# Dividing the attention keys into two parts where they are computed

## The chip, the cores and the metric

One core of one Trainium2 chip runs the kernel. The metric is device time in microseconds, from the first to the last instruction of one execution; several runs give a median. One more execution is taken with the hardware profiler, and it is the source of all rows below.

## The reference

The kernel computes one layer of a hybrid block for 1024 latent tokens and 256 context tokens of width 1024, all in float32. What matters here is the attention branch, with 8 heads:

```python
kv = (rms_norm(ckv, kv_norm_g) @ w_ukv).reshape(b, l, N_HEADS, QK_NOPE_DIM + V_HEAD_DIM)
k_nope, v = jnp.split(kv, [QK_NOPE_DIM], axis=-1)
...
k = jnp.concatenate([k_nope, k_pe], axis=-1)
...
s = jnp.einsum('bhqd,bhkd->bhqk', qi, k).astype(jnp.float32) * scale
p = jax.nn.softmax(s, axis=-1).astype(v.dtype)
return jnp.einsum('bhqk,bhkd->bhqd', p, v)
```

A head has 128 columns of k_nope and 64 rotated columns k_pe, which all heads share. Every latent token reads the 1280 keys of all tokens. Beside the attention there is a state-space branch (S5) with gates, and after both a retrieval layer (PEER): each token chooses 128 of 16384 experts, each a row of `peer_u` (scores) and a row of `peer_v` (values).

## The kernel before

**Numbers in two parts.** A score is a product of float32 numbers. The kernel forms it from parts in a shorter format (F32R): `split` (L230) casts x to a high part on ACT (L232) and subtracts it from x on an engine, VectorE by default, to get the low part (L233). A product is then three matmuls: high with high, low with high, high with low. In `attention`, L857 to L859 do so for the queries and the keys without rotation, and L860 and L861 add the rotated part from `kpe_h` and `kpe_l`, which are divided once, in `compress` (L688, L689).

**Stages.** First the S5 branch is computed, interleaved with the compression of all tokens (`compress`), the values (`values`) and the keys (`keys`). `keys(h, c0, c1)` (L701) makes one stretch of 512 or 256 keys of head h: two matmuls into a PSUM bank (L704), a copy to SBUF on ACT (L707), a store to the DRAM tensor `k_d` issued on ACT's queue (L708). There are 24 such calls. Their small buffers, tag `kv`, are a ring of 3 that `values` and earlier steps also use. PSUM tiles of the tag `mm` alternate between two banks at most.

Then the 8 tiles of 128 latent tokens go through in four groups, of 1, 2, 3 and 2 tiles (`GROUPS`, L42). A group's `front` (L1402) runs attention, gates, the output projection with its norms (`close`), and hands back the generator of its retrieval choice (`route`), whose steps are taken between the heads of the next group's attention (`TSTEP`, two steps per head). The gathers of expert rows for tiles 0 and 1 (`score`, L1269 and L1273; `weighted`, L1349 and L1354), which POOL issues, are emitted after the last front, with a lower priority, and fill in beside groups 1 to 3. Tiles 2 to 5 are served at the end by a dense stage over all experts (L1233 to L1235, L1194 to L1196), with the gathers of tiles 6 and 7 beside it.

**Attention, head by head.** For each pair of heads the query weight is loaded and the queries computed (L816 to L830). For each head the 1280 keys are loaded from `k_d` (L837), by `wload` (L203), into the ring W: 4 buffers of 8 KB per partition that are handed out in program order, for query weights, keys, the retrieval's query weights (L1052) and gate weights alike. A buffer is free again when the last reader of its former load is done. Then the keys are divided in three stretches (L839 to L844) into six tiles, one buffer each, in the pool of the attention; the values are loaded into a ring of two (L846); and for each token tile come the 15 score matmuls, three maxima on VectorE (L862), three exponentials on ACT (L871), and, one step later, transposes and the product with the values (`finish`, L795).

**The order.** All loads are issued on SP's queue, stores mostly on ACT's; each queue and engine works in order. The order within each is set when the program is built, by a scheduler that simulates a timeline, with priorities (`PRIO`, L69). Tiles of a pool have fixed addresses; a tile may be filled when whatever held these addresses before has been read for the last time, so that the attention pool's loads wait for pools that were released before it.

Of the kernel before, what the change touches and what calls it, by code (L numbers as in the profile page):

```python
# [8 lines left out]
F32 = mybir.dt.float32  # L9
F32R = mybir.dt.float32r  # L10
# [7 lines left out]
MUL, ADD, SUB = ALU.mult, ALU.add, ALU.subtract  # L18
# [4 lines left out]
KEYS = 1280  # L23
# [58 lines left out]
KENG = ((), (), (), ())  # L82
# [6 lines left out]
def block_kernel(ctx: ExitStack, tc: tile.TileContext, a: dict, out: bass.AP):  # L89
# [35 lines left out]
    k_d = tc.dram_tile([8, 128, KEYS], F32, name="k_d")  # L125
# [104 lines left out]
    def split(hi, lo, x, eng=V):  # L230

        S.copy(hi, x)  # L232
        eng.tensor_tensor(lo, x, hi.bitcast(F32), op=SUB)  # L233
# [39 lines left out]
    mrow = pre.tile([128, 512], F32, tag="kv", bufs=3, name="mrow")  # L273
# [27 lines left out]
    def project(n):  # L301
# [25 lines left out]
        su = pre.tile([128, 4, 128], F32, tag="kv", bufs=3, name="su")  # L327
# [363 lines left out]
    def values(n):  # L691
        for h in range(2):
            ps = bank("mm", "pv")
            for k in range(2):
                PE.matmul(ps, ckvT[:, k, n * 128:(n + 1) * 128], wk[k][:, 1024 + h * 512:1536 + h * 512],
                          start=(k == 0), stop=(k == 1))
            vt = pre.tile([128, 512], F32, tag="kv", bufs=3, name="vt")
            S.copy(vt, ps)
            S.dma_start(v_d[4 * h:4 * h + 4, :, n, :].rearrange("h p d -> p h d"), vt.rearrange("p (h d) -> p h d", h=4))

    def keys(h, c0, c1):  # L701
        ps = bank("mm", "pk")
        for k in range(2):
            PE.matmul(ps[:, 0:c1 - c0], wk[k][:, h * 128:(h + 1) * 128], ckvT[:, k, c0:c1],  # L704
                      start=(k == 0), stop=(k == 1))
        kt = pre.tile([128, 512], F32, tag="kv", bufs=3, name="kt")
        S.copy(kt[:, 0:c1 - c0], ps[:, 0:c1 - c0])  # L707
        S.dma_start(k_d[h, :, c0:c1], kt[:, 0:c1 - c0])  # L708
# [79 lines left out]
    def attention(grp, att):  # L788
# [22 lines left out]
        for pr in range(4):  # L811
# [19 lines left out]
            for hh in range(2):  # L831
# [5 lines left out]
                kt = wload(k_d[h], [128, KEYS])  # L837
                kc = []
                for c in range(3):  # L839
                    c0, w = 512 * c, (512 if c < 2 else 256)  # L840
                    kh = A.tile([128, w], F32R, tag="kh%d" % c, name="kh")
                    kl = A.tile([128, w], F32R, tag="kl%d" % c, name="kl")
                    split(kh, kl, kt[:, c0:c0 + w], GP if c in KENG[GROUPS.index(grp)] else V)
                    kc.append((kh, kl))  # L844
# [745 lines left out]
```

## Time and profile before

| what | us |
|---|---|
| median of 3 runs | 3764.03 (3756.9 to 3764.93) |
| profiled execution, its own time | 3758.78 |
| span of the profiled execution, first to last instruction | 3757.0 |
| mean granted TensorE clock in it | 0.946 of full speed |

Engines are PE (matmul), PEld (its weight loads), DVE (VectorE), ACT (ScalarE), POOL (GpSimd) and SP (which only issues loads). Busy time is the time in which an engine executes. "a <- b: 12.3, 4" in a list of waits says that a's instructions sat idle for 12.3 us in 4 cases until b was done. The chain is followed back from the last instruction to what released each piece of work. A piece of it shows its start, its length in us and what it was; "issue" is time without a visible cause.

### The profile page before, as it was taken

How to read it: one execution, taken by the hardware profiler on the slowest of the kernel's cores; microseconds unless marked ns; L12 is line 12 of the kernel's file. 1: busy time of each engine (PE TensorE's matmuls, PEld its weight loads, DVE VectorE, ACT ScalarE, POOL GpSimd, SP SyncE). 2: the span in 40 equal slices, each digit the busy share in tenths (PEclk: the TensorE clock that was granted, in tenths of full speed). 3: DMA queues.
4: the chain of work that ended last, by engine and by line, in shares of the span. 5: the costliest groups of instructions: out<-in, count | busy, mean ns of one | idle time of the engine just before them, and what ended most of it. 6: DMA issues, size and time to landing. Idle time of an engine off the chain costs nothing.

```text
span 3757.0 us, 54909 instructions
## 1 busy us (share of the span) xinstructions
PE 3376.1 (90%) x20022; PEld 2741.5 (73%) x20022; DVE 2889.2 (77%) x6864; ACT 1496.5 (40%) x2967; POOL 1477.3 (39%) x1254
## 2 busy tenths in 40 slices
PE   5968888979779889879989879999999999999997
PEld 3745577869667669667659668788888888888885
DVE  7357755685898877789846667888888888889985
ACT  2223353443123457133359794333333333333332
POOL 5035400041355553454441300465555555546530
PEclk7978999989889989989999989999999999999998
DMA  8652276476698888887887854699999999989972
GB/s 279 230 87 72 89 263 225 157 296 244 230 341 312 311 334 334 339 325 286 292 328 272 323 206 163 236 359 339 343 336 337 332 335 339 340 319 355 338 272 73
DMA packets 348718, 1032.49 MB, mean 275 GB/s; under 512 B 46592, under 2 KB 142080, under 8 KB 322592
## 3 DMA queue, kind: packets, MB, share of 16 engines
q0 software_dynamic: 147456, 536.94, 39.0%
q1 hardware_dynamic: 164032, 462.20, 34.7%
q10 hardware_dynamic: 36960, 29.86, 2.5%
q8 instruction: 157, 2.57, 0.3%
q14 instruction: 113, 0.93, 0.1%
HBM read 961.27 MB, written 67.62 MB: 274 GB/s over the span
## 4 chain that ended last, share of the span: by engine, by line
PE 56%; DVE 9%; issue 7%; DMA 5%; ACT 4%; POOL 2%; SPq 0%; DVEq 0%; ACTq 0%; POOLq 0%
PE turn L1233 6%; PE turn L1234 6%; PE turn L1235 6%; PE fd L1194 5%; PE fd L1195 5%; PE fd L1196 5%; DMA ub<-in_peer_u,ei 2%; PE pqr L1065 2%; DVE ub L1273 2%; PE acc L1354 2%; PE pe L1151 2%; DMA vb<-in_peer_v,eiT 2%; PE po L808 2%; PE po L953 1%; POOL ub L1269 1%
## 5 line engine op out<-in xcount | busy, mean ns | idle before, releaser
L1269 POOL DMA_INDIRECT ub<-in_peer_u,ei x512 | 639.6, 1249 | 1221.7 <-DVE ub L1273 446.8
L1273 DVE SCALAR_TENSOR_TENSOR ub<-ub,h 128x1024 f32<-128x1024 f32 x512 | 617.0, 1219 | 52.4 <-DMA ub<-in_peer_u,ei 46.5
L1316 POOL DMA_INDIRECT vb<-in_peer_v,ei x256 | 363.4, 1420 | 266.3 <-DVE f L1319 203.6
L1349 POOL DMA_INDIRECT vb<-in_peer_v,eiT x256 | 288.4, 1126 | 402.8 <-PE acc L1354 313.5
L1233 PE MATMUL turn<-hh,u 128*128 128x512 f32 x1024 | 400.9, 392 | 1.2 <-ACT act L1237 1.2
L1234 PE MATMUL turn<-hh,u 128*128 128x512 f32 x1024 | 400.5, 391 | 0.1
L1235 PE MATMUL turn<-hl,u 128*128 128x512 f32 x1024 | 399.9, 390 | 0.0
L1195 PE MATMUL fd<-v,kpe_l 128*128 128x512 f32 x891 | 353.5, 397 | 3.6 <-DVE kpe_l L233 3.6
L1196 PE MATMUL fd<-v,kpe_h 128*128 128x512 f32 x891 | 351.1, 394 | 0.0
L1194 PE MATMUL fd<-v,kpe_h 128*128 128x512 f32 x891 | 341.5, 397 | 0.0
L1319 DVE SCALAR_TENSOR_TENSOR f<-vb,zz,f 128x1024 f32<-128x1024 f32 x254 | 325.7, 1282 | 3.1 <-DMA vb<-in_peer_v,ei 0.4
L1237 ACT ACTIVATE act<-turn 128x512 f32<-128x512 f32 x128 | 76.6, 598 | 588.0 <-PE turn L1235 587.9
L232 ACT CAST v<-w 128x1024 fp32r<-128x1024 f32 x128 | 134.8, 1053 | 282.9 <-PE fd L1195 279.4
L1233 PEld LDWEIGHTS turn<-hh,u 128*128 128x128 f32 x1024 | 192.2, 188 | 44.1 <-ACT act L1237 1.4
L1235 PEld LDWEIGHTS turn<-hl,u 128*128 128x128 f32 x1024 | 192.3, 188 | 41.9
L1234 PEld LDWEIGHTS turn<-hh,u 128*128 128x128 f32 x1024 | 192.2, 188 | 41.1 <-DVE u L233 0.4
L1354 PE MATMUL acc<-vb,diag 128*32 128x256 f32 x2048 | 164.5, 402 | 49.0 <-DMA vb<-in_peer_v,eiT 45.8
L1148 DVE TENSOR_SCALAR second<-iota,pl 128x128 f32<-128x128 f32 x512 | 141.4, 350 | 81.4 <-PE pe L1151 74.7
L1195 PEld LDWEIGHTS fd<-v,kpe_l 128*128 128x128 f32 x891 | 167.5, 188 | 43.4 <-DVE kpe_l L233 4.6
L1196 PEld LDWEIGHTS fd<-v,kpe_h 128*128 128x128 f32 x891 | 167.6, 188 | 41.5
L1194 PEld LDWEIGHTS fd<-v,kpe_h 128*128 128x128 f32 x891 | 167.3, 188 | 40.7
L233 DVE TENSOR_TENSOR v<-w,v 128x1024 fp32r<-128x1024 f32 x128 | 156.6, 1223 | 43.4 <-ACT v L232 42.7
(422 smaller groups left out, 8254.2 us busy)
## 6 DMA issues: line engine op xcount, KB each, us to landing
w<-in_peer_uT SPq DMA_DIRECT2D x64, 1024.0 KB
w<-in_peer_v SPq DMA_DIRECT2D x64, 1024.0 KB
w<-in_peer_wq SPq DMA_DIRECT2D x32, 1024.0 KB
gT_d<-stage SPq DMA_DIRECT2D x16, 2048.0 KB
gt<-gT_d SPq DMA_DIRECT2D x32, 1024.0 KB
vh<-v_d SPq DMA_DIRECT2D x32, 640.0 KB
w<-k_d SPq DMA_DIRECT2D x32, 640.0 KB
w<-in_w_mod_b SPq DMA_DIRECT2D x16, 1024.0 KB
```

Of the source, the lines that this page charges most:

```text
L1194: PE.matmul(o, ah[:, ts], vh[:, cs], start=first, stop=False)
L1195: PE.matmul(o, al[:, ts], vh[:, cs], start=False, stop=False)
L1196: return PE.matmul(o, ah[:, ts], vl[:, cs], start=False, stop=final)
L1233: PE.matmul(turn, uh[:, k, :], hh[:, k, :], start=(k == 0), stop=False)
L1234: PE.matmul(turn, ul[:, k, :], hh[:, k, :], start=False, stop=False)
L1235: PE.matmul(turn, uh[:, k, :], hl[:, k, :], start=False, stop=(k == 7))
L1269: GP.indirect_dma_start(out=ub, out_offset=None, in_=a["peer_u"], in_offset=bass.IndirectOffsetOnAxis(ap=ei[:, s:s + 1], axis=0))
L1273: V.scalar_tensor_tensor(ub, ub, 1.0, h2, op0=MUL, op1=MUL, accum_out=dots[:, s:s + 1])
L1316: GP.indirect_dma_start(out=vb, out_offset=None, in_=a["peer_v"], in_offset=bass.IndirectOffsetOnAxis(ap=ei[:, s:s + 1], axis=0))
L1319: V.scalar_tensor_tensor(f, vb, z[:, s:s + 1], f, op0=MUL, op1=ADD)
L1349: GP.indirect_dma_start(out=vb, out_offset=None, in_=a["peer_v"], in_offset=bass.IndirectOffsetOnAxis(ap=eiT[:, t:t + 1], axis=0))
L1354: PE.matmul(acc[d // 2][o:o + 32, 256 * (d % 2):256 * (d % 2) + 256], dg[:, q, jj, :], vb[:, d * 256:(d + 1) * 256], start=False, stop=Fal ...
```

## The change

`keys` now makes two tiles per call: ACT casts the PSUM bank into the high part, VectorE subtracts it from the bank into the low part, and both are stored, so that `k_d` has a dimension of 2 and twice the size. The ring `kv` grows to 4 buffers. In `attention` the six tiles and their casts and subtractions are gone. In groups 0 to 2 (`KTB`, which takes the place of `KENG`) one load per head fetches both parts into a ring of two tiles of its own, in the attention's pool: 20 KB per partition where the six tiles had 10 KB. In group 3 two loads per head fetch the parts into two buffers of the ring W, and the matmuls read them there.

```diff
-KENG = ((), (), (), ())
+KTB = (2, 2, 2, 0)
...
-    k_d = tc.dram_tile([8, 128, KEYS], F32, name="k_d")
+    k_d = tc.dram_tile([8, 128, 2, KEYS], F32, name="k_d")
...
-            vt = pre.tile([128, 512], F32, tag="kv", bufs=3, name="vt")
+            vt = pre.tile([128, 512], F32, tag="kv", bufs=4, name="vt")
...
-        kt = pre.tile([128, 512], F32, tag="kv", bufs=3, name="kt")
-        S.copy(kt[:, 0:c1 - c0], ps[:, 0:c1 - c0])
-        S.dma_start(k_d[h, :, c0:c1], kt[:, 0:c1 - c0])
+        for z in range(2):
+            kt = pre.tile([128, 512], F32, tag="kv", bufs=4, name="kt")[:, 0:c1 - c0]
+            if z:
+                V.tensor_tensor(kt.bitcast(F32R), ps[:, 0:c1 - c0], kh, op=SUB)
+            else:
+                kh = kt
+                S.copy(kt.bitcast(F32R), ps[:, 0:c1 - c0])
+            S.dma_start(k_d[h, :, z, c0:c1], kt)
...
-                kt = wload(k_d[h], [128, KEYS])
-                kc = []
-                for c in range(3):
-                    c0, w = 512 * c, (512 if c < 2 else 256)
-                    kh = A.tile([128, w], F32R, tag="kh%d" % c, name="kh")
-                    kl = A.tile([128, w], F32R, tag="kl%d" % c, name="kl")
-                    split(kh, kl, kt[:, c0:c0 + w], GP if c in KENG[GROUPS.index(grp)] else V)
-                    kc.append((kh, kl))
+                ktb = KTB[GROUPS.index(grp)]
+                if ktb:
+                    kt = A.tile([128, 2, KEYS], F32R, tag="kt", bufs=ktb, name="kt")
+                    SY.dma_start(kt.bitcast(F32), k_d[h])
+                    kt = kt[:, 0], kt[:, 1]
+                else:
+                    kt = [wload(k_d[h, :, z], [128, KEYS]).bitcast(F32R) for z in range(2)]
+                kc = [[x[:, c:min(c + 512, KEYS)] for x in kt] for c in range(0, KEYS, 512)]
```

## Rows read from the trace of the kernel before

**Rows 1.** The page, busy us (share of the span) xinstructions of each engine.

```profile
PE 3376.1 (90%) x20022; PEld 2741.5 (73%) x20022; DVE 2889.2 (77%) x6864; ACT 1496.5 (40%) x2967; POOL 1477.3 (39%) x1254
```

**Rows 2.** Windows: from:to, length, busy PE PEld DVE ACT POOL, PEclk, DMA share, GB/s.

```profile
290.00:430.00 140.00, 122.63 (x645) 76.59 (x644) 116.29 (x169) 48.94 (x123) 86.12 (x98) 0.88 0.23 69
430.00:475.00 45.00, 37.80 (x187) 24.34 (x186) 28.97 (x48) 18.05 (x42) 5.81 (x4) 1.00 0.40 134
...
488.00:550.00 62.00, 56.35 (x377) 51.01 (x375) 35.21 (x99) 39.64 (x105) 0.00 (x0) 0.93 0.71 250
...
640.00:805.00 165.00, 142.46 (x958) 126.84 (x957) 122.36 (x467) 72.83 (x207) 23.24 (x20) 0.96 0.53 188
...
1000.00:1305.00 305.00, 255.34 (x1845) 205.86 (x1843) 273.64 (x948) 100.19 (x262) 164.64 (x151) 0.93 0.88 323
...
1765.00:1915.00 150.00, 139.66 (x1114) 99.96 (x1116) 118.86 (x543) 54.15 (x139) 67.31 (x64) 0.97 0.81 286
...
2400.00:3000.00 600.00, 595.99 (x2569) 481.64 (x2568) 523.70 (x715) 198.85 (x270) 349.04 (x255) 1.00 0.94 339
```

**Rows 3.** The chain that ended last, shares by line.

```profile
by line: issue 7.4%; PE turn L1233 6.0%; PE turn L1234 5.9%; PE turn L1235 5.9%; PE fd L1194 5.3%; PE fd L1195 5.3%; PE fd L1196 5.3%; DMA ub<-in_peer_u,ei 2.5%; PE pqr L1065 2.5%; DVE ub L1273 2.4%; PE acc L1354 2.0%; PE pe L1151 1.9%; DMA
```

**Rows 4.** Tile kh: xcount: ns min/median/max, first and last start us, forms.

```profile
L232 ACT CAST kh<-w x96: 399/618/660, 488.9 to 1891.5; 128x512 fp32r<-128x512 f32 x64, 128x256 fp32r<-128x256 f32 x32
L233 DVE TENSOR_TENSOR kl<-w,kh x96: 409/681/736, 489.6 to 1893.7; 128x512 fp32r<-128x512 f32 x64, 128x256 fp32r<-128x256 f32 x32
```

**Rows 5.** Tile kt, its stores; and the page's DMA issues, KB each.

```profile
L708 ACTq DMA_DIRECT2D k_d<-kt x24: 326/336/462, 300.9 to 472.6; - x24
...
w<-k_d SPq DMA_DIRECT2D x32, 640.0 KB
```

**Rows 6.** Lines 689 and 604 alone, columns as in group 4.

```profile
L689 DVE TENSOR_TENSOR kpe_l<-pt,kpe_h x5: 278/292/292, 321.6 to 447.6; 128x128 fp32r<-128x128 f32 x5
...
L604 DVE TENSOR_TENSOR gi<-w1t,w2t x8: 824/1027/1885, 235.3 to 455.3; 128x640 f32<-128x640 f32 x8
```

**Rows 7.** The chain in group 1, pieces with keys: start us, us, what.

```profile
647.16 1.44 ACT kh L232 x3
...
681.31 4.14 DMA w<-k_d
...
686.00 0.92 ACT kh L232 x2
...
732.63 3.98 DMA w<-k_d
...
766.16 0.66 DVE kl L233
...
770.47 0.33 DVE kl L233
```

**Rows 8.** DVE's groups, 1000 to 1305 us: xcount | busy, mean ns | idle before.

```profile
L1273 DVE SCALAR_TENSOR_TENSOR ub<-ub,h 128x1024 f32<-128x1024 f32 x106 | 128.5, 1217 | 8.9 <-DMA ub<-in_peer_u,ei 8.6 <-issue 0.2
```

**Rows 9.** The chain in group 2, first and last of six kl pieces.

```profile
1068.72 0.59 DVE kl L233
...
1150.31 0.34 DVE kl L233
```

**Rows 10.** Waits of SP's queue, 475 to 2270 us: total, times, longest.

```profile
SPq L213 <- DVE kl L233: 137.6, 13, 31.0
```

**Rows 11.** Waits of DVE and of PE for gathered rows, 475 to 2270 us.

```profile
DVE ub L1273 <- DMA ub<-in_peer_u,ei: 34.1, 25, 4.5
...
PE acc L1354 <- DMA vb<-in_peer_v,eiT: 45.8, 21, 7.0
```

**Rows 12.** The window with the highest rate of those read, columns as in group 2.

```profile
1520.00:1565.00 45.00, 37.62 (x189) 29.81 (x188) 26.45 (x65) 1.19 (x2) 13.46 (x13) 0.89 0.92 351
```

**Rows 13.** Group 1's first value loads on SP; its first score matmuls on the chain.

```profile
647.14 0.80 SPq L846 DMA_DIRECT2D vh<-v_d  x2
...
657.47 0.59 PE pS L857 x3
```

More of the change, by code (lines that the diff above doesn't have):

```diff
@@ L272, in block_kernel @@
         SY.dma_start(ldt[64 * d:64 * d + 64, :], a["s5_log_dt"][d].partition_broadcast(64))
-    mrow = pre.tile([128, 512], F32, tag="kv", bufs=3, name="mrow")
+    mrow = pre.tile([128, 512], F32, tag="kv", bufs=4, name="mrow")
     GP.memset(mrow, 0.0)
@@ L326, in project @@
                 PE.matmul(pc[:, b, :], w1[:, k, b * 128:(b + 1) * 128], hm[:, k, :], start=(k == 0), stop=(k == 7))
-        su = pre.tile([128, 4, 128], F32, tag="kv", bufs=3, name="su")
+        su = pre.tile([128, 4, 128], F32, tag="kv", bufs=4, name="su")
         S.copy(su, pc)
```

## The prediction

> **What bounds the kernel now.** I read the busy line first: PE has the largest share, 90%, DVE 77%, ACT 40% [rows 1]. An average says little here, so I cut the span into stages [rows 2]; a reader should look for the engine whose busy time comes nearest to the stretch's own length. Keys are made up to 475 us; there DVE has 29.0 of the last 45 us. The four attention stages follow: group 0 (488 to 550), group 1 (640 to 805), group 2 (1000 to 1305) and group 3 (about 1625 to 1915). Group 0 is PE's, 56.4 of 62 us. Group 1 is PE's with DVE close, 142 and 122 of 165 us, and its DMA moves only 188 GB/s. Group 2 is DVE's, 273.6 of 305 us, at a DMA share of 0.88. The last part of group 3 is PE's again, 139.7 of 150 us. After that comes the dense stage, in which PE is never idle (596 of 600 us). Then the chain of what ended last [rows 3]: its largest lines are the dense stage's matmuls; gathers and the score multiplication of L1273 follow; nothing of the keys' division reaches the list. The change touches nothing in the dense stage, so all that it can win or lose lies before it.
>
> **What is removed.** 96 casts kh on ACT (median 0.618 us) and 96 subtractions kl on DVE (0.681 us), two thirds 512 and one third 256 wide [rows 4]. Per group that is 24 of each: 16 x 0.681 + 8 x 0.41 = 14.2 us of DVE, and 16 x 0.618 + 8 x 0.40 = 13.1 us of ACT. Over four groups DVE loses 57 us and ACT 52 us. ACT is not the fullest engine in any of these stages [rows 2], so its 52 us count only where they stand on the chain.
>
> **What is added.** In the keys' stage, per call one more DVE subtraction from PSUM and one more store. The 24 stores are issued on ACT's queue at 0.336 us [rows 5], 8 us on an engine busy 18 of 45 us. In the attention, every head reads 1280 KB in place of 640 KB [rows 5]: 5.24 MB more per group, 21 MB over four, and 5.24 MB more written once.
>
> **Keys' stage.** 16 subtractions of 512 and 8 of 256: 14.2 us by the durations of kl [rows 4]. No row shows this one exactly. The nearest is L689, the same operation with one input from PSUM, 128 wide: 0.278 to 0.292 us, five times, without spread [rows 6]. In the same stage L604, with both inputs in SBUF, goes from 0.824 to 1.885 us [rows 6], so another kind of DVE work is stretched there. Taking L689 as the nearer, I keep 14.2 us; stretched like L604's median against its minimum (1.25 times) it would be 18, like its maximum (2.3 times) 33. In the last 45 us DVE has 16 us free; before that it has 24 of 140 [rows 2]. The PSUM bank of each call is also held until the subtraction ends, and the next matmul of that bank waits for that. I put under half of it on the path: **+6 us**, bounds 0 (all in DVE's free time) and +23 (most of the stretched case).
>
> **Group 0.** Its casts and subtractions lie beside PE, which leaves 62 - 56 = 6 us to win at most. The loads go from 250 GB/s x 62 us = 15.5 MB to about 20.7 MB, 60 us at the 345 GB/s that the fullest stretches show (mean of 339 and 351 [rows 2, 12]). The next limit is as near as the old one: **0 us**, bounds -6 and +6.
>
> **Group 1.** Here the chain does touch the keys [rows 7]: twice it waits for a key load, 4.14 and 3.98 us, each time with 0.92 us of casts behind it; 1.44 us of casts stand on it at the first head, and three pieces of kl, 1.6 us, near the end. 8.1 + 1.8 + 1.4 + 1.6 is about 13 us. The load was late because it needs one of four buffers that it shares with the query and retrieval weights; in a ring of its own, two heads deep, it starts a head earlier. What is late next is the value tile, which needs its ring too, or the route's matmuls, which already fill this stage. The first head is a place for a loss: value tiles, in the same pool as the new key tiles, are only issued at 647.14 [rows 13], and a key tile of twice the bytes takes some 8 us by rows 7, to 655; the first score matmul starts at 657.47 [rows 13]. It is covered with 2 us to spare. I take **-12 us**, bounds -13 and 0.
>
> **Group 2.** DVE is full, and 106 score multiplications of L1273 (128.5 us) share it with kl [rows 8]. Only two heads' kl, six pieces and 3.1 us, stand on the chain [rows 9]; but in an in-order queue that is 90% full the other pieces push what does. Between 3.1 and 14.2 us, nearer to the full engine: **-8 us**. Against it, 5.24 MB at 345 GB/s are 15.2 us of transfer, of which the stage has (345 - 323) x 305 us = 6.7 MB free. They fit, just. Bounds -14 and +8 (15.2 less the DVE time that goes).
>
> **Group 3.** The keys stay in the shared ring, as two tiles per head, kept until the head's last score matmul and no longer only until kl. kl and kh are not on the chain in this stage, PE is the fullest. I take **0 us**; bounds -6 (part of DVE's 14.2 while heads share it with routing) and +28 (the second rival).
>
> **The load queue.** On SP's in-order queue, loads into the shared ring waited 137.6 us in all for kl [rows 10]. In groups 0 to 2 this wait goes; the keys' own load will then wait for score matmuls two heads back, which is earlier in the queue than it bites. The chain shows no weight load that was late for it, so I count nothing.
>
> **Sum.** 6 + 0 - 12 - 8 + 0 = -14 us against the profiled execution's 3758.8 us (span 3757.0), or 3745. That execution stands 5.2 us under the median of the runs, 3764.0; on the median the sum gives 3750 us. Measurements of this kernel can tell about 0.2%, 7.5 us, from no change.
>
> **Rival one: the transfers take the gain back.** Before, DVE waited 34.1 us for gathered rows in its multiplications and PE 45.8 us for those of L1354, over groups 0 to 3 [rows 11]; both engines work in order, so a late row holds the attention behind it. The 15.7 MB of groups 1 to 3 are 46 us of transfer. If the DMA is what sets groups 2 and 3, group 2's -8 becomes 0 or more and group 3 adds a few: 6 - 12 + 0 + 4 = -2, that is 3762 us, no change. For it: shares of 0.81 to 0.92 and stretches at 339 to 351 GB/s and none higher [rows 2, 12]. Against it: group 1, with the surest gain, has 188 GB/s. In the Trainium skill, HBM Reference, section Specifications, a core's share is given as about 358 GB/s and a core alone as about 425; the trace, at 351, shows nothing above the share. By 425 group 2 would have 31 MB free instead of 6.7 and this rival would fall; by 358 it stands.
>
> **Rival two: the shared ring of group 3 (slower).** With two of four buffers per head, and two retrieval weights loaded between heads, the next head's key tile falls on the buffer of the last one, and can't be issued before its last score matmul; the next query weight likewise. A load costs the chain at least the 4.1 us of rows 7. Seven head changes: 7 x 4.1 = 28 us, and -14 becomes +14, or 3778 us. It decides once PE and DVE have less than 4 us of other work queued at each change. For it: nothing is prefetched across heads any more. Against: the routing of group 2 and the weighted rows of L1354 lie between heads and are PE's larger part here.
>
> **Rival three: the keys' stage pays in full.** +23 in place of +6 makes 3767, no change; with group 2 at 0 it is 3775, slower.
>
> **How the numbers follow.** Forecast, gains in groups 1 and 2: 0.44. Rival one 0.25; two 0.19; three 0.12, of which 0.02 stays within 0.2% and 0.10 is slower. So faster 0.44, same 0.27, slower 0.29. The range for 8 in 10 goes from 3722 (-42: nearly all lower bounds together, -6 - 13 - 14 - 6 = -39) to 3790 (rival two with one more bound, or three with part of two). The forecast's own range is 3722 to 3756.
>
> **What would show it.** Right: in the changed profile kh and kl are gone from the attention; the first score matmul of group 1 stands no later after its queries; no chain piece waits for a key load in group 1; group 2's stretch from first to last head is some 8 us shorter with the DVE busy time down by 14; the last k_d store and the start of group 0 are some 6 us later. Wrong: head-to-head gaps in group 3 with PE waiting on a load; DMA waits at L1273 and L1354 grown by more than 10 us; a dense stage that starts less than 8 us sooner than before.

## The result and the profile after

The changed kernel takes **3779.1 us** in the median (3774.7 to 3786.1, 6 runs), against 3759.1 us (3756.4 to 3764.9, 6 runs) for the kernel before on the same chip: a ratio of 1.0051, 95% interval 1.0033 to 1.0068. By the ratio it is slower by about 19 us, where 14 us of gain were forecast. Its profiled execution took 3777.1 us, with a span of 3774.7 us, 17.7 us above the span of before.

What the change was to do, it did. The page of the changed kernel, and, for the last line, its list of DMA issues:

```profile
PE 3378.2 (89%) x20022; PEld 2745.0 (73%) x20022; DVE 2849.5 (75%) x6792; ACT 1448.7 (38%) x2869; POOL 1471.0 (39%) x1254
...
kt<-k_d SPq DMA_DIRECT2D x24, 1280.0 KB
...
w<-k_d SPq DMA_DIRECT2D x16, 640.0 KB
```

Against [rows 1], DVE has 40 us less to do, ACT 48 us, PE the same. The 40 are roughly the 57 us of kl less the some 14 us that the subtraction in the keys' stage adds (tile kt of the changed kernel; ns min/median/max, first and last start):

```profile
L709 DVE TENSOR_TENSOR kt<-pk,kt x24: 418/678/692, 299.0 to 473.6; 128x512 fp32r<-128x512 f32 x16, 128x256 fp32r<-128x256 f32 x8
```

So the time was lost by work that waits, not by work that was added. I cut both spans at the same events of their timelines: the last matmul pa (end of the first query compression), a group's last `att` on ACT, the last matmul of `close`, the first `turn` of the dense stage. The numbers in this table are differences of those times, so each column adds up to its span. "Before, again" is a second profile of the same kernel on another chip (e5, the chip of e6) and shows how far one profile can be trusted: rows differ by up to 6 us. e1 and e2 ran on a third chip, on which the median of the kernel before is 3744.1 us, 15 us less; so a column of theirs can be read for where time moved, and not to the last few us against "before".

| stretch, us | before | before, again | changed | e1 | e2 | e6 |
|---|---|---|---|---|---|---|
| to the end of pa | 480.4 | 482.6 | 484.8 | 477.0 | 479.9 | 480.5 |
| to the end of group 0's attention | 91.2 | 89.1 | 99.9 | 89.4 | 99.9 | 96.8 |
| to the end of group 1's attention | 285.8 | 284.2 | 260.8 | 267.1 | 264.8 | 283.2 |
| to the end of group 1's close | 98.7 | 97.2 | 128.3 | 125.1 | 114.2 | 98.7 |
| to the end of group 2's close | 621.0 | 627.1 | 599.5 | 623.0 | 596.7 | 615.6 |
| to the end of group 3's close | 539.8 | 538.9 | 546.9 | 533.4 | 530.0 | 537.5 |
| to the dense stage | 153.4 | 150.9 | 173.0 | 156.6 | 167.9 | 147.9 |
| dense stage to the end | 1486.7 | 1483.8 | 1481.5 | 1483.4 | 1487.4 | 1489.3 |

In the changed kernel the attention of group 1 and all of group 2 are faster, by 25 and 21.5 us. Four stretches give more than that back: group 0 (+9), group 1's gates and close (+30), group 3 (+7) and what lies before the dense stage (+20). Group 3's 7 us are hardly more than the spread of the rows; the other three can be read in views.

**Group 0.** First the kernel before, SP's timeline (start us, us, what) and PE's (in brackets the idle time before it and what ended it); then the changed one, in the same order:

```profile
481.73 0.42 SPq L213 DMA_DIRECT2D w<-in_w_uq  x1
```

```profile
487.53 2.90 PE L820 MATMUL pq<-cqT,w 128*128 128x128 f32 x12 [2.30 <-issue]
```

```profile
479.03 0.48 SPq L845 DMA_DIRECT2D kt<-k_d  x1
479.56 0.42 SPq L851 DMA_DIRECT2D vh<-v_d  x1
480.03 0.43 SPq L845 DMA_DIRECT2D kt<-k_d  x1
...
489.38 5.05 SPq L213 DMA_DIRECT2D w<-in_w_uq  x4
```

```profile
501.32 5.28 PE L825 MATMUL pq<-cqT,w 128*128 128x128 f32 x24 [12.05 <-issue]
```

Now keys of two heads, in a ring of their own and so free to go, stand ahead of the first query weight, with the values and tables that used to follow it, and the queries start 14 us later; counted from the end of pa it is 9 us (16.5 in place of 7.1).

**Group 1.** ACT's timeline of the kernel before, then of the changed one, at the casts of the gates' inputs:

```profile
795.90 1.05 ACT L232 CAST hm<-w 128x1024 fp32r<-128x1024 f32 x1
804.07 1.04 ACT L232 CAST hm<-w 128x1024 fp32r<-128x1024 f32 x1 [3.16 <-DMA w<-hm_d]
```

```profile
845.49 1.05 ACT L232 CAST hm<-w 128x1024 fp32r<-128x1024 f32 x1
846.96 1.04 ACT L232 CAST hm<-w 128x1024 fp32r<-128x1024 f32 x1
866.41 1.90 ACT L232 CAST w<-w 128x2048 fp32r<-128x2048 f32 x1 [17.89 <-DMA w<-in_w_gm]
```

The last `att` of group 1 ends at 857.4 us in the first and at 845.5 in the second. Before, the casts were done over 50 us ahead of it; now the first one begins in the moment in which it ends. The attention's pool has become 10 KB longer and reaches into the addresses of the gates' pool, so the gates' tiles can be filled only when the attention is done. SP's timelines, before and changed, show what that does to the queue; the changed kernel's list of SP's waits, 800 to 860 us, and the waits of all engines, 820 to 900 us, show the price:

```profile
801.23 0.34 SPq L213 DMA_DIRECT2D w<-in_w_gm  x1
...
820.11 0.33 SPq L213 DMA_DIRECT2D w<-in_w_gm  x1
...
855.33 0.33 SPq L757 DMA_DIRECT2D hm<-hm_d  x1
```

```profile
845.22 0.32 SPq L762 DMA_DIRECT2D hm<-hm_d  x1
...
849.13 0.33 SPq L213 DMA_DIRECT2D w<-in_w_gm  x1
```

```profile
SPq L762 <- PE po L813: 32.1, 1, 32.1
```

```profile
PE pg L238 <- ACT w L232: 23.2, 1, 23.2
ACT w L232 <- DMA w<-in_w_gm: 17.9, 1, 17.9
```

The load L762, L757 before (for the next group's queries), waits for the attention's end in both kernels. Before, two of the gates' weights w_gm went out ahead of it. Now they stand behind it, and PE sits idle for 23 us in front of the gates. Read by itself, the attention of this group misleads: it is shorter because the gates' loads and casts no longer run beside it (e1 shows the same without any change of the keys).

**Group 2 and the rows behind it.** The attention went as forecast (the line of `att` in its group, before and after: 326 and 316 us from first to last):

```profile
L809 ACT ACTIVATE att<-po,smx x24: 350/368/373, 1023.0 to 1348.6; 128x128 f32<-128x128 f32 x24
```

```profile
L814 ACT ACTIVATE att<-po,smx x24: 367/367/386, 1030.3 to 1346.2; 128x128 f32<-128x128 f32 x24
```

But beside it DVE has to score 92 gathered rows of tile 0 in one stretch. DVE's groups in that stretch, before (985.3 to 1165.2 us) and after (1003.4 to 1201.2 us):

```profile
L1273 DVE SCALAR_TENSOR_TENSOR ub<-ub,h 128x1024 f32<-128x1024 f32 x92 | 111.1, 1216 | 5.0 <-DMA ub<-in_peer_u,ei 4.7 <-issue 0.2
L862 DVE TENSOR_REDUCE mx<-pS 128x1 f32<-128x512 f32 (+1 forms) x30 | 17.4, 593 | 2.9 <-PE pS L861 2.9
...
L994 DVE FIND_INDEX8 I<-V,sc 128x8 uint32<-128x128 f32 x19 | 5.3, 284 | 0.0
```

```profile
L1278 DVE SCALAR_TENSOR_TENSOR ub<-ub,h 128x1024 f32<-128x1024 f32 x92 | 111.1, 1215 | 5.1 <-DMA ub<-in_peer_u,ei 4.8 <-issue 0.3
L867 DVE TENSOR_REDUCE mx<-pS 128x1 f32<-128x512 f32 (+1 forms) x36 | 20.2, 592 | 7.1 <-PE pS L866 7.1
...
L999 DVE FIND_INDEX8 I<-V,sc 128x8 uint32<-128x128 f32 x24 | 6.7, 284 | 0.0
```

The rows cost the same 111.1 us and wait the same 5 us for their gathers. There is more other work between them: 36 maxima for 30, 24 searches of L999 for 19. The attention and the choice of experts go ahead, the score rows fall behind: they take 198 in place of 180 us. They end 36 us later, and the other half of that is their later start, with group 1's close 18 us late. The weighted rows (L1354, now L1359) come behind them through the same six buffers and the same queue on POOL. Their matmuls from 1640 us on, before and after:

```profile
L1354 PE MATMUL acc<-vb,diag x1344: 379/379/636, 1652.5 to 2165.1; 128*32 128x256 f32 x192
```

```profile
L1359 PE MATMUL acc<-vb,diag x1392: 376/379/637, 1646.6 to 2242.5; 128*32 128x256 f32 x199
```

They end 77 us later, 123 in place of 49 us after group 3's close, and the dense stage starts 23 us later (its first matmuls, before and after):

```profile
L1233 PE MATMUL turn<-hh,u x77: 387/389/504, 2270.3 to 2399.9; 128*128 128x512 f32 x77
```

```profile
L1238 PE MATMUL turn<-hh,u x62: 389/389/628, 2293.2 to 2400.0; 128*128 128x512 f32 x62
```

Much of the 20 us ahead of it is PE's work that used to be done earlier. PE's groups of row matmuls between group 3's close and the dense stage, before (2116.9 to 2270.3 us) and after (2120.2 to 2293.2):

```profile
L1354 PE MATMUL acc<-vb,diag 128*32 128x256 f32 x188 | 14.5, 390 | 2.6 <-DMA vb<-in_peer_v,eiT 2.5
```

```profile
L1359 PE MATMUL acc<-vb,diag 128*32 128x256 f32 x368 | 29.4, 411 | 7.2 <-DMA vb<-in_peer_v,eiT 6.1 <-issue 1.1
```

These are 180 more, 15 us of PE; 48 of them used to be done in group 2's stretch of the table and 132 in group 3's. DVE's work is put off too. The stretches of group 2 and group 3 in the table, before and after (columns as in [rows 2]):

```profile
956.10:1577.10 621.00, 530.69 (x3891) 444.41 (x3891) 507.56 (x1503) 251.83 (x581) 295.62 (x262) 0.93 0.86 316
1577.10:2116.90 539.80, 487.63 (x3797) 385.76 (x3799) 402.17 (x1516) 286.41 (x637) 214.69 (x190) 0.95 0.82 303
```

```profile
973.80:1573.40 599.60, 529.44 (x3841) 446.84 (x3840) 478.32 (x1443) 239.65 (x557) 280.96 (x242) 0.94 0.87 320
1573.40:2120.20 546.80, 482.47 (x3673) 386.45 (x3674) 409.78 (x1531) 276.62 (x620) 204.12 (x188) 0.94 0.83 306
```

In each of the two groups 14 us of kl are gone. Yet DVE's busy time (the third of the busy times) falls by 29 us in group 2 and grows by 8 in group 3: some 15 us of other work left group 2, and some 22 came to group 3. That the rows did not wait longer for transfers is shown by their waits from 475 to 2270 us; [rows 11] had 34.1 and 45.8:

```profile
PE acc L1359 <- DMA vb<-in_peer_v,eiT: 48.4, 25, 9.3
...
DVE ub L1278 <- DMA ub<-in_peer_u,ei: 24.2, 18, 4.6
```

### The profile page after: what moved, and what is told of

The parts are those of the page before. It is cut to its first block, busy times and chain, and to the rows that moved or that the text cites. A ratio compares the mean times of both kernels' runs of the same rounds, so it can differ in the third digit from the quotient of the medians.

```text
span 3774.7 us, 54757 instructions
## 1 busy us (share of the span) xinstructions
PE 3378.2 (89%) x20022; PEld 2745.0 (73%) x20022; DVE 2849.5 (75%) x6792; ACT 1448.7 (38%) x2869; POOL 1471.0 (39%) x1254
## 4 chain that ended last, share of the span: by engine, by line
PE 63%; DVE 16%; issue 9%; DMA 6%; ACT 4%; POOL 1%; ACTq 0%; SPq 0%; another core or an unknown queue 0%; DVEq 0%; POOLq 0%
PE turn L1239 6%; PE turn L1238 6%; PE turn L1240 6%; PE fd L1199 5%; PE fd L1200 5%; PE fd L1201 5%; DVE ub L1278 3%; PE po L813 2%; PE pqr L1070 2%; PE acc L1359 2%; DMA ub<-in_peer_u,ei 2%; DMA vb<-in_peer_v,eiT 2%; PE pe L1156 2%; PE pt L809 1%; PE pq L825 1%
## 5 line engine op out<-in xcount | busy, mean ns | idle before, releaser
L1274 POOL DMA_INDIRECT ub<-in_peer_u,ei x512 | 650.6, 1271 | 1164.9 <-DVE ub L1278 449.7
L1354 POOL DMA_INDIRECT vb<-in_peer_v,eiT x256 | 273.8, 1070 | 493.6 <-PE acc L1359 381.3
L1242 ACT ACTIVATE act<-turn 128x512 f32<-128x512 f32 x128 | 76.5, 597 | 596.7 <-PE turn L1240 596.7
L1359 PE MATMUL acc<-vb,diag 128*32 128x256 f32 x2048 | 167.7, 406 | 50.7 <-DMA vb<-in_peer_v,eiT 48.4
L233 DVE TENSOR_TENSOR v<-w,v 128x1024 fp32r<-128x1024 f32 x128 | 156.6, 1223 | 40.0 <-ACT v L232 38.6
```

What stands on the lines that cost most here:

```text
L1274: GP.indirect_dma_start(out=ub, out_offset=None, in_=a["peer_u"], in_offset=bass.IndirectOffsetOnAxis(ap=ei[:, s:s + 1], axis=0))
L1354: GP.indirect_dma_start(out=vb, out_offset=None, in_=a["peer_v"], in_offset=bass.IndirectOffsetOnAxis(ap=eiT[:, t:t + 1], axis=0))
L1359: PE.matmul(acc[d // 2][o:o + 32, 256 * (d % 2):256 * (d % 2) + 256], dg[:, q, jj, :], vb[:, d * 256:(d + 1) * 256], start=False, stop=Fal ...
```

## The experiments

Theories at the outset: the room taken in group 1's pool; the order of loads in group 0; the shared ring in group 3; the added bytes. A fifth came last: the order in which the instructions stand in the queues, which is worked out anew for every version. Ratios are to the kernel before on the same chip, with 95% intervals.

**e1, the room alone.** The kernel before, with a tile of 10 KB in group 1's attention pool that nobody uses:

```diff
+                if h == 0 and grp == GROUPS[1]:
+                    A.tile([128, 2 * KEYS], F32, tag="pad", name="pad")
```

> The kernel before, with an unused tile of 10 KB per partition ahead of the value tiles in group 1's attention pool: the extra room that the change takes there, and nothing else of it. Theory A (room): the pool then reaches into the addresses of group 1's gates, whose first casts hm, at 795.9 us in the kernel before, must wait for the attention's last read; they come at its end, some 50 us later, the gates start 15 to 30 us later, and the whole is 10 to 25 us slower than before (3769 to 3784). Theory B (transfers): only the bytes and the load order count; casts hm at 796 us and the time of before, within 7 us.

Measured: 1.0037 (1.0019 to 1.0055), 14 us. ACT's timeline of e1:

```profile
833.14 0.37 ACT L809 ACTIVATE att<-po,smx 128x128 f32<-128x128 f32 x1 [1.48 <-PE po L808]
833.40 1.03 ACT L232 CAST hm<-w 128x1024 fp32r<-128x1024 f32 x1
...
851.35 1.90 ACT L232 CAST w<-w 128x2048 fp32r<-128x2048 f32 x1 [14.93 <-DMA w<-in_w_gm]
```

The same picture as in the changed kernel, without any of its work: casts at the attention's end, weights late. It also shows the false gain: the attention is 19 us shorter in the table's third line and the close takes 26 us longer in the fourth, +8 together. Where the rest of the 14 us lies, the table doesn't show. Its matmuls stand in the order of before until 817 us, so up to the collision nothing else differs.

**e2, no tile of its own in group 1.** Keys of group 1 go through the shared ring, as in group 3: `KTB = (2, 0, 2, 0)`.

> The changed kernel with group 1's keys in the shared ring as group 3's are, so that its attention pool has 10 KB less than before and not 10 KB more. Theory A: the casts hm of group 1 come before its attention ends again, the gates follow within 5 us, and 15 to 30 us of the 20 lost come back: 3750 to 3765. Theory B: the same bytes are moved, so 3775 to 3785.

Measured: 1.0020 (1.0009 to 1.0031). Three fifths of the loss are gone, 12 us, a little less than the 15 to 30 that were expected. Group 1 now takes 379.0 us from group 0's attention to its close, against 389.1 in the changed kernel and 384.5 before: a gain of 5 us at most, on a faster chip, where 12 were forecast.

**e3, one buffer.** `KTB = (1, 1, 1, 0)`: each ring of its own is one tile, and the attention's pool has the length of before.

> The changed kernel with one key tile in place of two in groups 0 to 2: the attention pools have the size of before, and a head's keys can only be loaded when the head before has been scored. Theory A: the gates of group 1 start right at its attention's end, but each head waits for its load, 6 to 8 us in group 0: group 0's attention 20 to 50 us longer; in all 3770 to 3800. Theory B: gates of group 1 late as in the changed kernel, and the loads spread less: 3790 or more.

Measured: 1.0065 (1.0039 to 1.0090). Without the second tile a head's load waits for the last head's matmuls, and group 1's attention is 191 us long from first to last `att`, 182 before. The room is gone as a cause and another wait has come: SP holds the key loads back for 173 us in all until score matmuls are done (SP's waits, 475 to 2270 us).

**e4, query weight first.** In group 0 the first key load of each pair of heads is bound behind the last query weight.

```diff
-                    SY.dma_start(kt.bitcast(F32), k_d[h])
+                    with tc.issue_after(last[0].ins) if grp == GROUPS[0] and hh == 0 else nullcontext():
+                        SY.dma_start(kt.bitcast(F32), k_d[h])
```

> The changed kernel with group 0's first key load of each pair put behind the pair's query weight in the load queue. In the changed kernel PE waited 12 us for that weight, behind two key tiles, two value tiles and five tables. If the order of the loads is what group 0 lost at its start, its queries begin 8 to 10 us earlier (at 491 to 494, not 501 us) and the whole is up to 10 us faster, 3768 to 3777; if the bytes themselves are the cause, the queries come no earlier than 498 us and the time stays at 3779 within 5.

Measured: 1.0057 (1.0040 to 1.0073), no better. The first queries come 11.9 us after pa in place of 16.5 (7.1 before), and nothing of it reaches the end. The order is not all of it: the weight is issued at 483.36 and its matmuls start 11.8 us later, where 5.8 us were enough before; the key loads of twice the size are issued right behind it.

**e5, the kernel before once more,** for the spread of one profile.

> The kernel before once more, for a profile from the chip of the next three. Casts hm of group 1 ahead of the attention's end and the last weighted row (L1354) at about 2165 us less the start's shift; time as before within 0.3%.

Measured: 3755.5 us; see the table.

**e6, the high part alone.** As e2, with only the high part of the keys loaded and used for both products. The low part's load and use are left out, so a head reads 640 KB as before.

```diff
-                    SY.dma_start(kt.bitcast(F32), k_d[h])
-                    kt = kt[:, 0], kt[:, 1]
+                    SY.dma_start(kt[:, 0].bitcast(F32), k_d[h, :, 0])
+                    kt = kt[:, 0], kt[:, 0]
...
-                    kt = [wload(k_d[h, :, z], [128, KEYS]).bitcast(F32R) for z in range(2)]
+                    kt = [wload(k_d[h, :, 0], [128, KEYS]).bitcast(F32R)] * 2
```

> As the run with group 1's keys in the shared ring, but only the high part of the keys is loaded and used in place of both, with one buffer of the shared ring per head: what is left out is the low part's load (the products with it read the high part). Its keys' stage is that of the change, its loads those of before. Theory bytes or theory ring (both parts' transfers, or the second buffer, are what kept the gain away): 0.991 to 0.997 of before. Theory start (what is left of the loss lies in the keys' stage and in the order of group 0's first loads): 1.000 to 1.003, and the queries of group 0 begin as late as in the changed kernel, 12 us after the first product pa or more.

Measured: 0.9990 (0.9977 to 1.0002). That lies between its two expectations; against e2 it is 0.3%. Its last weighted row starts at 2157.6 us, e2's at 2191.9. This speaks for the bytes, but the matmuls of the two come in another order from the first group on, so it is no proof.

**e7, the shared ring at full pressure.** e6, with a second buffer of the ring taken per head in groups 1 and 3, filled with 128 KB only.

```diff
+                    kt = wload(k_d[h, :, 0], [128, KEYS]).bitcast(F32R)
+                    kc = [[kt[:, c:min(c + 512, KEYS)]] * 2 for c in range(0, KEYS, 512)]
+                    kc[2] = kc[2][0], wload(k_d[h, :, 1, 1024:KEYS], [128, 256]).bitcast(F32R)
```

> As the run before this, but in groups 1 and 3 the head takes its second buffer of the shared ring, with a load of 128 KB in place of 640; only the last 256 keys' low part is real, for the rest the high part is used in its place. Theory bytes: as fast as the run with the high part alone, within 0.2%. Theory ring: as slow as the run with group 1's keys in the shared ring, 1.001 to 1.004.

Measured: 0.9994 (0.9982 to 1.0006), like e6. Two buffers per head in group 3 cost nothing that can be measured.

**e8, a tile of its own in group 3.** `KTB = (2, 0, 2, 1)`.

> The changed kernel with group 1 in the shared ring and group 3 with one key tile of its own in the attention's pool. Theory ring: the shared buffers of group 3 are free again, the weighted rows end 15 to 30 us sooner than in the run with group 1 in the shared ring, ratio 0.994 to 0.999. Theory bytes or start: 1.001 to 1.004, no change to it.

Measured: 1.0044 (1.0029 to 1.0059), no better than e2. This says little about the ring: with one tile per head, as in e3, a load waits for the last head's score matmuls. Against the second rival stand e7 and the changed kernel's own waits: in PE's list from 1640 to 1935 us, which holds group 3's attention, no load of keys appears; the longest, 18.9 us in ten pieces, is for gathered rows.

**e9, bytes added to the kernel before.** Each head of groups 1 to 3 gets a copy of its 640 KB of keys to a scratch store.

```diff
+                if grp != GROUPS[0]:
+                    SY.dma_start(dump_d[GROUPS.index(grp), h], k_d[h])
```

> The kernel before, in which every head of groups 1 to 3 also copies its 640 KB of keys to an unused place in DRAM: the change's extra traffic in these groups, and nothing else of it. Theory bytes (from the runs with one and with both parts): the 128 score rows of tile 0 end 10 to 16 us later and the whole is 0.2 to 0.4% slower, 1.002 to 1.004. Rival (transfers hide in what the DMA has free): within 0.1% of before, the score rows as before within 4 us.

Measured: 1.0086 (1.0059 to 1.0113), and no answer. Nothing held the copies back: all 24 went out between 464 and 505 us, and the end of pa came 29 us late, while groups 1 to 3 got no extra bytes at all. e13 repeats it with the copies in place.

**e10, e2 and e4 together.**

> The changed kernel with group 1's keys in the shared ring (no extra room) and group 0's first key load behind the query weight. If the room, the load order and the bytes are the three parts of the loss, the first is gone and half of the second: queries of group 0 start 4 to 5 us sooner than without the order, and the ratio is 0.999 to 1.002, with the bytes' part left. If the background gathers alone set the end, the order brings nothing again: 1.001 to 1.004.

Measured: 1.0016 (0.9999 to 1.0033), which fits both expectations. Of the two causes that can be seen in the trace the room is out, and the delay of the first queries is down to 10.3 us after pa. What is left is at the edge of what can be measured; of the forecast gain there is none.

**e11 and e12, fewer weighted rows.** The last 32 of tile 1's 128 weighted rows are left out, in the changed kernel (e11) and in the kernel before (e12).

```diff
-            for b in range(8):
+            for b in range(6 if l == 1 else 8):
```

> The changed kernel without the last 32 of 128 value rows of tile 1 in the gathers beside the front (L1354's kind): that part of tile 1's retrieval is left out. Theory late gathers (groups 2 and 3 of the front win, the gathers behind them lose, and their rows that are still open after the front set the start of the dense stage): the dense stage starts 15 to 25 us sooner than in the changed kernel, ratio 0.998 to 1.001. Rival (the front's own last steps, L1151's kind, set that start): 1.003 to 1.005.

> The kernel before with the same 32 rows of tile 1 left out. Theory late gathers: there the gathers end 105 us ahead of the dense stage, so less comes of it than in the changed kernel, 0 to 8 us: 0.998 to 1.000. Rival: the same in both, whatever it is.

Measured: e11 0.9999 (0.9979 to 1.0019), e12 0.9967 (0.9947 to 0.9987). Without these rows the changed kernel is 0.5% faster and the one before 0.3%, 12 us, more than the 0 to 8 that were expected there; in the profiles the stretch ahead of the dense stage is 27 and 17 us shorter. The matmuls stand in their old order up to the rows left out in both, so the rows' work counts at the end in both kernels. That it does so more in the changed one is what the two profiles say; the intervals of the two effects overlap. And it isn't shown that the rows' lateness is what counts: 256 matmuls are left out with them, in the changed kernel 21 us of PE's busy time (167.7 to 146.7 for L1359).

**e13, the bytes in place.** e9, with each copy bound directly behind its head's key load (`with tc.issue_after(last[0].ins):`).

> The kernel before, with a copy of 640 KB from the keys' store to a scratch store bound directly behind each head's key load in groups 1 to 3 (24 copies, results used by nobody). If the added bytes themselves take the gain back, the score rows of tile 0 (180 us before, 198 in the changed kernel) take 190 us or more, the weighted rows end later after group 3's close than the 49 us of before, and the ratio is 1.002 to 1.004 or above. If it is the order of the queues and not the bytes, the score rows stay within 4 us of 180 and the ratio is 0.999 to 1.001.

Measured: 1.0057 (1.0038 to 1.0075); 92 score rows in 201 us; DVE waits longer for gathered rows than the 34.1 us of [rows 11] (waits of e13, 475 to 2270 us):

```profile
DVE ub L1277 <- DMA ub<-in_peer_u,ei: 49.5, 34, 4.1
```

Its weighted rows end 85 us after group 3's close. By its expectation this shows the bytes. e17 takes that back for the time, though not for the score rows.

**e14, three costs away.** e6 and e4 together: no room, no late query weight, no added bytes in the loads (the low part left out as in e6).

> The changed kernel with three costs away: no key tile of its own in group 1, only the high part of the keys loaded and used for both products (the low part's load and use are left out), and group 0's first key load of each pair issued behind the last query weight. If the loss is made of room, load order and bytes, the gain that was predicted for the engines appears: 0.997 or less. If the engines' time that the change frees has no worth of its own because other work sets the end, the ratio stays at 0.998 to 1.001, as without the change of load order (0.9990).

Measured: 0.9984 (0.9971 to 0.9998), 6 us faster (1 to 11). That is inside the second expectation (0.998 to 1.001), at its lower end. The engines' time that the change frees is worth some 6 us here, less than half of the 14. e14 and e6 have all their matmuls in the same order, and the first queries come 10.3 and 13.5 us after pa; their ratios differ by 0.06% and their intervals overlap, so these 3 us of group 0 don't show at the end.

**e15 and e16, earlier score rows.** e10 (e15) and the kernel before (e16), with 64 in place of 36 of tile 0's score rows ahead of their hold (`S0 = 64`). The hold is a bond in the program that keeps the rest of the rows behind the first query compression of group 2.

> The changed kernel without a key tile of its own in group 1, with group 0's query weight ahead of the keys, and with 64 in place of 36 of tile 0's score rows ahead of their hold. If the gain in group 2's front is lost because the score rows then come too late for the weighted rows, taking 28 more of them early gives it back: 0.998 or less, against 1.0016 without. If the bytes set the stage, it stays at 1.000 to 1.003.

> The control: the kernel before with 64 in place of 36 score rows ahead of the hold. If the earlier rows are of use only where the change has freed group 2's front, the ratio is 1.000 to 1.003. If they help any version, it is 0.998 or less here too, and what the run beside it shows says nothing on the change.

Measured: e15 0.9992 (0.9978 to 1.0005), e16 1.0000 (0.9986 to 1.0015). e16 fell as a control should. e15 lies between its two expectations, 0.24% under e10 with intervals that overlap, so the late score rows are at most a part of what is left. e15 is the best version with the low part complete; it is level with the kernel before.

**e17 and e18, the same order, no bytes.** As e13, with copies of 512 bytes (e17) and of 2560 bytes in 640 packets of 4 bytes (e18).

```diff
-                        SY.dma_start(dump_d[GROUPS.index(grp), h], k_d[h])
+                        SY.dma_start(dump_d[GROUPS.index(grp), h, :, 0:1], k_d[h, :, 0:1])
```

In e18 it is `0:10:2` in place of `0:1`.

> As e13, with copies of 512 bytes (128 packets of 4 bytes) in place of 640 KB. Nearly nothing is moved, but the engines' queues have another order than before. If e13's loss is the transfers' own, this is 0.999 to 1.001 and the score rows of tile 0 stay within 4 us of 180. If it is the order, this loses a good part of e13's 0.57%: 1.003 or more, and score rows of 190 us or more.

> The same order of every engine as e17, copies of 2560 bytes in 640 packets of 4 bytes each, which keep the DMA engines busy for a time in place of moving bytes (the trace gives the dose). If the time that transfers take from the gathered rows is what costs, this is slower than e17 by 0.2% or more and DVE waits longer for gathered rows; if not, the two are within 0.1% of one another.

Measured: e17 1.0052 (1.0031 to 1.0073), e18 1.0069 (1.0048 to 1.0090). 24 copies of 512 bytes cost as much as 24 of 640 KB, as the expectation had it for the order. But they cost it in another place than expected: in e17 the 92 score rows take 180 us as before, and the weighted rows end 44 us after group 3's close (tile ub of e17, and the matmuls of its weighted rows from 1640 us on):

```profile
L1277 DVE SCALAR_TENSOR_TENSOR ub<-ub,h x92: 1203/1215/1274, 981.5 to 1159.8; 128x1024 f32<-128x1024 f32 x92
```

```profile
L1358 PE MATMUL acc<-vb,diag x1344: 379/379/637, 1640.6 to 2175.0; 128*32 128x256 f32 x192
```

Against the two profiles of the kernel before, the loss is in group 2 (+9 and +3 us), group 3 (+9 and +10) and the stretch ahead of the dense stage (+6 and +8). The matmuls of e17 follow the order of before until 1023 us and another one from there. Either that order costs the time, or the issues themselves, 24 of 0.48 us on SP, 11 us in all:

```profile
L841 SPq DMA_DIRECT2D dump_d<-k_d x24: 475/476/2127, 617.7 to 1835.7; - x24
```

The two weren't told apart. In either case e13's time is no proof for the bytes: its loss has the size that an edit without bytes has too.

What the bytes do go with is the delay of the score rows. The 92 rows take 188 to 201 us in the eight kernels that load or copy the added bytes in group 2 (the changed one, e2, e3, e4, e8, e10, e11, e13), and 180 to 186 in the ten that don't (before, e1, e5, e6, e7, e9, e12, e14, e17, e18); e15 and e16 hold another number of rows back. How it comes about is open, as DVE's waits for gathered rows are longer in e13 and shorter in the changed kernel, and so is its price at the end, since e17 loses as much without it. e18 and e17 have all 20,022 matmuls in the same order, and differ by the copies alone; the DMA queue of SP (share of 16 engines' span), e17 and e18:

```profile
q1 hardware_dynamic: 167488, 462.21, 34.8%
```

```profile
q1 hardware_dynamic: 179776, 462.26, 35.3%
```

That is 0.353 x 3779.7 - 0.348 x 3772.4 = 21 us of all DMA engines' time, for 6 us in the median. That is between the 0.1% and the 0.2% of its expectation, and the intervals overlap. DVE's wait for gathered rows is 38.8 us in e18 and 43.0 in e17, against what was expected; PE's, which no expectation named, is 60.2 and 49.9. So a price of transfers at an unchanged order is likely and not shown, and its size is open: between the two profiles of the kernel before, the same queue's time differs by some 8 us.

## Why the prediction was wrong

Two steps failed. The term of group 1 took 12 us of gain and looked for the price of the longer pool in the wrong place; and the sum had no term for the retrieval's rows, which run on between group 3's close and the dense stage.

**The keys' stage** was sized rightly: +6 forecast, +4 in the table (+2 against the second profile of before), the subtraction at 0.678 us as kl was [rows 4], no stretching. Rival three falls.

**Group 0, forecast 0, cost 9.** "The next limit is as near as the old one" looked at the bytes of the whole stage. What counted was the first 20 us: loads that had shared a ring with the query weight got a ring of their own and went ahead of it. How much of the 9 us reaches the end isn't shown: e4, e10 and e14, which take back 3 to 6 of them, differ by no more than 0.06% from the same kernels without that edit.

**Group 1, forecast -12, cost 5.** Two errors. The 8 us of waits for keys and the casts on the chain [rows 7] were not worth 12. As forecast, no piece of the changed kernel's chain in this stage (640 to 800 us) waits for a key load. But PE, the fullest engine, had not sat idle for keys: its list of waits, kernel before, 640 to 805 us, has no key load and no cast of keys, and starts with the exponentials:

```profile
PE pS L857 <- ACT P L871: 8.3, 4, 3.4
```

Where the room doesn't interfere, group 1 gains 5 us (e2) or 3 (e6; against e5, from e6's own chip, nothing), and the two profiles of before differ by 3. And "covered with 2 us to spare" looked for the price of the longer pool at the stage's start; it stood at the end, where the next pool's tiles wait for the same addresses. It is the one cause whose wait the trace shows and that a run brings about by itself (e1: +14 us in all, 8 of them in group 1).

**Group 2, forecast -8, gained 21.** The attention is 10 us shorter, near the forecast. Another 10 us lie ahead of its first head, between group 1's close and the first `att` (956.1 to 1023.0 before, 973.8 to 1030.3 after), a stretch that no term of the sum looked at. And beside kl some 15 us of DVE's work are put off from this group to later ones, as its windows above show. So the gain stands in the right place, and the 13 us by which it is larger than forecast come from what the term didn't have. DVE's busy time from 1000 to 1305 us fell by 7.5 us, not 14, against [rows 2]; of the 24 pieces of kl only 18 had lain in that window before, 10.7 us:

```profile
1000.00:1305.00 305.00, 263.03 (x1838) 212.12 (x1838) 266.15 (x942) 93.70 (x255) 158.29 (x140) 0.94 0.88 324
```

**Group 3, forecast 0, cost 7, and the stretch ahead of the dense stage, not in the sum, cost 20.** This is where group 2's gain went. I summed stages as if each ended with its own work. The retrieval's rows run across them, through one set of buffers, one queue on POOL and two engines that work in order, and the dense stage is near them: 32 rows fewer shorten the stretch ahead of it by 17 us even before the change (e12). The attention and the choice of experts went ahead, the rows came 77 us later, and 15 us of their matmuls moved into this stretch. Whether the queues' order or the bytes put them off is not shown.

**The load queue, forecast 0.** The wait for kl went [rows 10], and its like came in its place, the loads of keys behind the matmuls of the head before the last (waits of SP in the changed kernel, 475 to 2270 us):

```profile
SPq L845 <- PE pS L866: 161.5, 16, 25.2
```

**The rivals.** Rival two named 3778 us, and 3779 was measured; still it is wrong. Its mechanism costs nothing that can be measured (e7), PE never waits for a key load in group 3, and group 3's attention grew by 4 us, not 28. The match is luck also in the sum, which started from 3764.0, the median of three runs, and not from 3759.1. A right time is no evidence for a mechanism. Rival one's sign, longer waits for gathered rows, is absent (24.2 and 48.4 us for 34.1 and 45.8), though the score rows do fall behind in all kernels with the added bytes. The prediction also said that no stretch is above 351 GB/s. The page has one, and had one before (359); this is the changed kernel's rate by slice:

```profile
GB/s 279 234 84 88 122 297 227 220 271 235 236 330 310 326 358 304 346 351 311 284 319 276 307 282 177 219 362 342 342 337 341 334 333 339 336 317 357 340 273 73
```

The slice at 362 GB/s lies in the dense stage. Shorter windows move more, in the kernel before too (columns as in [rows 2]):

```profile
796.00:836.00 40.00, 21.87 (x114) 18.79 (x113) 34.16 (x63) 17.17 (x34) 22.04 (x16) 0.70 1.02 411
```

So the 345 GB/s by which groups 0 and 2 were bounded are the mean of two stretches and no limit. The Trainium skill (HBM Reference, Specifications) gives about 358 GB/s as a core's share and about 425 for a core that streams alone; the 362 and the 411 agree with the second figure, as one core ran here. In group 2 the rate stayed where it was, 324 GB/s after 323, so the trace doesn't say what would bound it there. Of the signs listed, the one that spoke was the last: the dense stage starts 23 us later in place of 8 us sooner.

**What stays open.** Room is worth about 12 of the 19 us by e2 against the changed kernel, 14 by e1; in group 1's own rows of the table it is 10 and 8. The rest, with the 6 us that the engines gain (e14), is bytes, order, or both. e6, e14 and the score rows put it at the bytes; e17 shows that an edit that moves next to nothing can cost as much.

## What to carry to other kernels

Before a tile grows or gets a ring of its own, look at both ends of its pool: who filled these addresses early, and what stands behind the load that will wait for them. A stage's gain counts only when the work that runs across the stages keeps up, so follow that chain to the stage that needs it. Where the order of the queues is worked out anew for each version, run a control that moves nothing: here 0.5% was the price of 24 copies of 512 bytes, and a difference of that size says nothing on bytes, engines or buffers until a trace shows the wait.

## What was not expected of the hardware

A copy of 512 bytes from DRAM to DRAM takes SP 0.476 us to issue, one of 640 KB in e13 0.473, and one of e18 with 640 packets of 4 bytes 0.542: the size didn't matter to the issue. And packets of 4 bytes go with far more DMA time than their bytes would: e18 has 12,288 more of them than e17, 0.05 MB, and its queue took 21 us more of all 16 engines, where the 21 MB that the changed kernel loads in addition took 0.359 x 3774.7 - 0.347 x 3757.0 = 51 us. By the trace's packet times the small packets themselves are 7 of the 21 us, some 9 ns each; of the rest, 13 us are the queue's packets of 2 KB and more, which are as many as in e17 and took longer. Some of that is spread, as the same queue's time differs by some 8 us between the two profiles of the kernel before.
